# Half two's up-projections and the down-projection of a decoder step by Strassen's scheme

## The chip, the cores and the metric

The kernel runs on one core of a Trainium2 chip. The metric is the device time of one execution in microseconds. Five engines work side by side, each through its own list of instructions in order: TensorE (PE in the profile; its weight loads are a separate line, PEld), VectorE (DVE), ScalarE (ACT), GpSimd (POOL) and SyncE (SP), on whose queue this kernel issues all of its transfers. They hand over by semaphores.

## What is computed

One step of a decoder layer for 2048 prompt tokens and 8 sequences of 4 sample tokens, in float32. Only the end of the layer matters here: a gated feed-forward block (model width 1024, hidden width 2816) behind the token mixer and its output projection, and a last norm.

```python
x = x + g1 * (o @ p['w_out'][l])
h = _rmsnorm(x, p['norm_ffn'][l]) * (1 + sc2) + sh2
gate, b_ffn = _causal_dwconv(h @ p['ffn_w_gate'][l], b_ffn, p['ffn_conv_w'][l])
gate = gate + p['ffn_conv_b'][l]
x = x + g2 * ((jax.nn.silu(gate) * (h @ p['ffn_w_up'][l])) @ p['ffn_w_down'][l])
...
y = _rmsnorm(x, final_norm)
```

## The kernel before, in words

Every dense product is float32 made from three passes: both operands are split into a high part in the type float32r (a cast on ScalarE) and a low part, what is left (a subtraction on VectorE, `raw - hi`), and TensorE adds high·high, high·low and low·high in PSUM. A matmul has a stationary operand of 128 x 128 and a moving one of up to 512 columns.

The tokens go in two halves of 1024. The list of dense blocks that `drive` (L97) walks is `A0 + A1 + B0 + C0 + B1 + C1`: input projections of the halves, output projection of half one (B0), up-projections of half one (C0), output projection of half two (B1), up-projections of half two (C1). The recurrences are woven in as background work up to the end of C0. Behind the list comes `ffn_down` (L1802).

- **B1** (`wout`, L1634). Token tiles of 128 rows; the output weight lies on chip as three groups of columns in the "ring". For each tile the product goes times the gate on VectorE (L1682), plus the residual on GpSimd (L1683), to DRAM as `x1` (L128, the store helper), and is then normed, transposed on TensorE (`prep_turn`, L508) and stored as `h2T`, features by tokens.
- **C1** (`ffn_up`, L1745). The ring holds the half's normalised tokens in three groups of 384, 384 and 256+32 columns (`load_group`, L555, loads them from `h2T`, casts and subtracts). For each of 22 blocks of 128 hidden features there are two weights, gate and up; for each group of tokens `fgroup` (L590) issues 8 x 3 matmuls (L598 to L600). The gate goes through a convolution (`conv_evac`, L656: copies on ScalarE and GpSimd, two multiply-adds on VectorE), tanh and multiply (L652, L653), and times the up product (L1767) it is stored as `aT`.
- **Down** (`ffn_down`). Two passes over all 16 token tiles, each with 11 of the 22 row blocks of `w_down` on chip, 512 columns wide. `a_raw` is loaded, cast (L1899) and subtracted (L1900) per tile; `down_mm` (L1793) issues the matmuls (L1797 to L1799). A tile's sum goes times the gate (L1917, VectorE), plus `x1` (L1918, GpSimd), back to `x1` in pass one, and through the last norm (L1848, L158, L159, L1858) to the output in pass two. The 32 sample rows have products of their own (L1818).

Order in an engine's list is settled when the program is built: code order, rearranged by a scheduler that runs its own estimate of a timeline. Waits are on semaphores between tiles' writers and readers.

Of the kernel before, what the change touches and what calls it, by code (L numbers as in the profile page):

```python
# [31 lines left out]
# groups of tokens (first token, tokens, samples' tokens) of the two halves: the samples go through the input  # L32
# projection with the first half and through the rest with the second
# [11 lines left out]
RA = 4 * (32 * 256 + 32)    # room of a chunk: its four diagonal blocks and the next chunk's are equally far apart  # L45
# [3 lines left out]
class Block:  # L49
    """dense work that shares weight units: loaders of the units, slots of products, what goes between them"""  # L50
# [16 lines left out]
class Kern:  # L67
    def __init__(self, ctx, tc, ins, outs):
        self.ctx, self.tc, self.nc = ctx, tc, tc.nc
        self.i = ins  # L70
        self.o = outs
        self.dram = {}
        self.queue = []
        self.clock = 0
        self.bg = [[], []]      # background work, on the two sides
        self.acc = [0.0, 0.0]
        self.rate = (0, 0)
        self.R = [None] * 3

    # ---------------------------------------------------------------- background and dense work  # L80
# [9 lines left out]
    def finish(self, gens):  # L90
        """emit the background work up to the end of gens"""
# [5 lines left out]
    def drive(self, blocks):  # L97
        """dense blocks, their units loaded ahead, the background work woven in"""
# [24 lines left out]
    # ---------------------------------------------------------------- helpers  # L123
# [6 lines left out]
    def later(self, n, fn):  # L130
        """emit fn behind the n-th next slot of dense products"""
# [23 lines left out]
    def rpow(self, out, in_, n, scale, m):  # L155
        """out = (in*scale + eps) ** -0.5 on small tiles"""
# [4 lines left out]
    # ---------------------------------------------------------------- set up  # L161
    def setup(self):
# [3 lines left out]
        self.pstat = ctx.enter_context(tc.tile_pool(name="pstat", bufs=1, side="left"))  # L166
        self.pw = ctx.enter_context(tc.tile_pool(name="pw", bufs=3, side="left"))
# [35 lines left out]
    def setup2(self):  # L203
        """parameters needed first"""
# [4 lines left out]
        def rows(name, spec):  # L209
            """parameters as rows of 128, transposed on the chip into columns"""  # L210
# [19 lines left out]
    def setup3(self):  # L230
        """masks, the other parameters, persistent states"""
# [7 lines left out]
        self.tri = pc.tile([128, 128], F32, name="tri")  # L239
        nc.gpsimd.affine_select(out=self.tri, in_=self.ones, pattern=[[1, 128]], compare_op=ALU.is_ge,  # L240
                                fill=0.0, base=0, channel_multiplier=-1)
        # blk4[s, t] = 1 in the same block of four tokens; tri4 = blk4 * (s <= t)
        self.tri4 = pc.tile([128, 128], F32, name="tri4")
# [6 lines left out]
        self.blk4 = pc.tile([NS, NS], F32, name="blk4")  # L250
        nc.gpsimd.tensor_copy(self.blk4, self.tri4[:NS, :NS])
        nc.gpsimd.tensor_tensor(self.tri4, self.tri4, self.tri, op=ALU.mult)
        self.neg = pc.tile([128, 128], F32, name="neg")
        nc.vector.tensor_scalar(self.neg, self.tri, 1.0, -NEG, op0=ALU.subtract, op1=ALU.mult)
        self.neg4 = pc.tile([128, 128], F32, name="neg4")
        nc.vector.tensor_scalar(self.neg4, self.tri4, 1.0, -NEG, op0=ALU.subtract, op1=ALU.mult)
        # masks of the HGRN levels in blocks of 32 tokens: second halves as columns, first halves as partitions
        self.lmask = {}
        def quarters(name, src, n):
            """the blocks of n columns on the diagonal of src, under one another"""  # L260
            d = pc.tile([128, n], F32, name=name, tag=name)
# [5 lines left out]
        for h in (1, 2, 4, 8, 16):  # L267
            nb = 64 // h
            m = self.pw.tile([128, 520], F32, name="lm_f", tag="raw", bufs=NRAW)[:, :64]
# [8 lines left out]
        # sel[:, b] = ones in column b  # L278
        self.sel = pc.tile([128, 8, 32], F32, name="sel")
# [13 lines left out]
        # conv weights of the half-argument (silu(x) = y (1 + tanh y), y = x / 2)  # L293
# [3 lines left out]
        # persistent conv halos and states  # L297
        self.halo = pc.tile([128, 14, 3], F32, name="halo")
# [3 lines left out]
        self.sconv = pc.tile([128, 14, 24], F32, name="sconv")  # L302
# [5 lines left out]
        self.Shg = [pc.tile([128, 2, 128], F32, name=f"Shg{n}", tag=f"Shg{n}") for n in range(2)]  # L308
# [1917 lines left out]
```

## Time and profile before

| | |
|---|---|
| three runs, median (lowest to highest) | 2857.83 us (2856.66 to 2860.53) |
| the profiled execution, first to last instruction | 2864.5 us |
| TensorE busy | 2793.7 us, 98% |
| VectorE / ScalarE / GpSimd busy | 1582.8 / 1113.9 / 543.5 us |
| up-projections of half two (C1), from the last matmul of B1 to the first of down | 514.2 us |
| down-projection, to its last matmul | 512.9 us |

In rows of instructions the columns are start, duration, engine, line, operation, output<-inputs, shape and count; in square brackets stands how long the engine was idle before it and for whom. "Busy" of TensorE is a union of overlapping spans: a matmul of 512 columns has a span of about 0.39 us, but they start about 0.23 us apart, so what a matmul costs in a full stream is the distance between starts.

### The profile page before, as it was taken

The numbers are of one execution on the slowest core, as the hardware profiler recorded it, in microseconds if no ns is written. First come the engines' busy times: TensorE is split into PE (matmuls) and PEld (weight loads), VectorE is DVE, ScalarE is ACT, GpSimd is POOL, SyncE is SP. The second block draws the span as 40 slices with busy tenths as digits, with TensorE's granted clock in tenths as the row PEclk, the third lists the DMA queues.
The fourth block names the chain that finished last, engine by engine and source line by source line (L and its number), as shares of the span: only waits on it lengthen the run. The fifth ranks groups of instructions, "written<-read, shape, count | busy, mean of one in ns | idle before, by whom it ended". The sixth has DMA issues, their size and how long they took to land.

```text
span 2864.5 us, 52500 instructions
## 1 busy us (share of the span) xinstructions
PE 2793.7 (98%) x19657; PEld 2555.0 (89%) x19657; DVE 1582.8 (55%) x3434; ACT 1113.9 (39%) x2480; POOL 543.5 (19%) x1143
## 2 busy tenths in 40 slices
PE   7999999999999999999999999999999999999998
PEld 4999888889989999999999989999999997777777
DVE  4535776676576878565565546644434543325433
ACT  4544445445554545544443323432223331113111
POOL 3310222301113322111121102210000002111222
PEclk8999998999999999999999999999999999999999
DMA  6465336675556786553554345632222333345332
GB/s 232 146 201 154 115 108 184 187 214 142 170 177 185 235 271 194 158 153 114 179 160 112 100 142 171 186 100 69 70 68 82 100 114 123 104 141 174 98 117 96
DMA packets 521701, 418.59 MB, mean 146 GB/s; under 512 B 84566, under 2 KB 482806, under 8 KB 520422
## 3 DMA queue, kind: packets, MB, share of 16 engines
q1 hardware_dynamic: 521446, 415.24, 48.0%
q8 instruction: 154, 2.52, 0.4%
q14 instruction: 101, 0.83, 0.1%
HBM read 281.99 MB, written 133.14 MB: 145 GB/s over the span
## 4 chain that ended last, share of the span: by engine, by line
PE 66%; DMA 7%; DVE 3%; issue 1%; ACT 1%; SPq 1%; POOL 0%; DVEq 0%; POOLq 0%; ACTq 0%
PE mm_f L598 13%; PE mm_f L600 13%; PE mm_f L599 13%; PE mm_d L1797 5%; PE mm_d L1799 5%; PE mm_d L1798 5%; DMA rb<-rows 1%; DMA w_raw<-oT 1%; SPq L125 1%; DMA h_raw<-h2T 1%; DMA h_raw<-in_w_out_dram 1%; DMA kq<-qkvT 1%; PE kvt L1031 1%; DMA d_raw<-in_ffn_w_down_dram 1%; PE ssq L717 1%
## 5 line engine op out<-in xcount | busy, mean ns | idle before, releaser
L598 PE MATMUL mm_f<-g_hi,w_hi 128*128 128x384 f32 (+2 forms) x3072 | 1005.8, 327 | 4.2 <-ACT g_hi L569 4.0
L600 PE MATMUL mm_f<-g_hi,w_lo 128*128 128x384 f32 (+2 forms) x3072 | 995.1, 324 | 0.0
L599 PE MATMUL mm_f<-g_lo,w_hi 128*128 128x384 f32 (+2 forms) x3072 | 994.0, 324 | 0.3 <-DVE g_lo L570 0.2
L598 PEld LDWEIGHTS mm_f<-g_hi,w_hi 128*128 128x128 f32 x3072 | 581.1, 189 | 26.0 <-issue 14.8
L599 PEld LDWEIGHTS mm_f<-g_lo,w_hi 128*128 128x128 f32 x3072 | 581.3, 189 | 6.6 <-issue 4.8
L600 PEld LDWEIGHTS mm_f<-g_hi,w_lo 128*128 128x128 f32 x3072 | 581.3, 189 | 6.4 <-issue 5.7
L546 DVE TENSOR_TENSOR w_lo<-w_raw,w_hi 128x512 fp32r<-128x512 f32 (+1 forms) x328 | 228.0, 700 | 132.6 <-ACT w_hi L545 127.6
L545 ACT CAST w_hi<-w_raw 128x512 fp32r<-128x512 f32 (+1 forms) x328 | 201.1, 619 | 240.7 <-PE mm_f L599 196.4
L1797 PE MATMUL mm_d<-d_hi,a_hi 128*128 128x512 f32 (+1 forms) x715 | 282.9, 396 | 1.2 <-ACT d_hi L1789 1.2
L1798 PE MATMUL mm_d<-d_lo,a_hi 128*128 128x512 f32 (+1 forms) x715 | 278.7, 390 | 0.5 <-DVE d_lo L1790 0.5
L1799 PE MATMUL mm_d<-d_hi,a_lo 128*128 128x512 f32 (+1 forms) x715 | 278.6, 390 | 0.0
L671 DVE SCALAR_TENSOR_TENSOR uy<-cv_u,par,uy 128x384 f32<-128x384 f32 (+1 forms) x264 | 151.5, 574 | 196.8 <-ACT uy L668 169.2
L663 ACT COPY cv_u<-mm_f 128x384 f32<-128x384 f32 (+1 forms) x216 | 95.3, 441 | 332.0 <-PE mm_f L600 330.5
L1899 ACT CAST a_hi<-a_raw 128x512 fp32r<-128x512 f32 (+1 forms) x96 | 55.9, 585 | 357.4 <-DMA a_raw<-aT 265.7
L673 POOL COPY fhalo<-cv_u 128x2 f32<-128x2 f32 x132 | 39.8, 301 | 745.2 <-ACT cv_u L663 738.9
L1900 DVE TENSOR_TENSOR a_lo<-a_raw,a_hi 128x512 fp32r<-128x512 f32 (+1 forms) x96 | 68.5, 718 | 193.1 <-ACT a_hi L1899 193.0
L1797 PEld LDWEIGHTS mm_d<-d_hi,a_hi 128*128 128x128 f32 x715 | 134.3, 188 | 38.6 <-issue 4.9
L1799 PEld LDWEIGHTS mm_d<-d_hi,a_lo 128*128 128x128 f32 x715 | 134.5, 188 | 31.1
L1798 PEld LDWEIGHTS mm_d<-d_lo,a_hi 128*128 128x128 f32 x715 | 134.4, 188 | 30.2 <-DVE d_lo L1790 1.3
L1918 POOL TENSOR_TENSOR d_y<-d_y,d_x 128x512 f32<-128x512 f32 x62 | 89.8, 1468 | 369.0 <-DVE d_y L1917 369.0
L641 PE MATMUL mm_t<-w_hi,g_hi 128*128 128x260 f32 (+1 forms) x544 | 141.3, 295 | 4.4 <-ACT g_hi L1967 4.4
L671 DVE SCALAR_TENSOR_TENSOR qy<-cv_u,par,qy 128x384 f32<-128x384 f32 (+1 forms) x216 | 122.8, 572 | 38.5 <-POOL cv_u L662 23.5
(514 smaller groups left out, 4461.3 us busy)
## 6 DMA issues: line engine op xcount, KB each, us to landing
w_raw<-in_w_in_dram SPq DMA_DIRECT2D x96, 256.0 KB
w_raw<-in_ffn_w_gate_dram SPq DMA_DIRECT2D x92, 256.0 KB
w_raw<-in_ffn_w_up_dram SPq DMA_DIRECT2D x92, 256.0 KB
aT<-uy SPq DMA_DIRECT2D x88, 192.0 KB
ada_w<-in_w_ada_dram SPq DMA_DIRECT2D x32, 512.0 KB
R<-recB SPq DMA_DIRECT2D x16, 1024.0 KB
a_raw<-aT SPq DMA_DIRECT2D x64, 256.0 KB
d_x<-x SPq DMA_DIRECT2D x32, 512.0 KB
```

What stands on the lines that cost most here:

```text
L545: nc.scalar.copy(hi[:, :n], raw[:, :n])
L546: nc.vector.tensor_sub(lo[:, :n], raw[:, :n], hi[:, :n].bitcast(F32))
L598: nc.tensor.matmul(ps[:, :N], wh, hi[:, k, :N], start=(k == 0), stop=False)
L599: nc.tensor.matmul(ps[:, :N], wh, lo[:, k, :N], start=False, stop=False)
L600: nc.tensor.matmul(ps[:, :N], wl, hi[:, k, :N], start=False, stop=(k == 7))
L641: nc.tensor.matmul(ps[:m, :nc_], a, wh[:, k % 2], start=(k == 0), stop=False)
L663: nc.scalar.copy(u[:, K:K + n], ps[:, :n])
L671: nc.vector.scalar_tensor_tensor(y[:, :n], u[:, j:j + n], cw[:, j, blk:blk + 1], y[:, :n], op0=ALU.mult, op1=ALU.add)
L1797: nc.tensor.matmul(d, a, hi[:, cs], start=(k == ks[0]), stop=False)
L1798: nc.tensor.matmul(d, a, lo[:, cs], start=False, stop=False)
L1799: nc.tensor.matmul(d, b, hi[:, cs], start=False, stop=(k == ks[-1]))
L1918: (nc.vector if last else nc.gpsimd).tensor_tensor(y[:, cs], y[:, cs], x[:, cs], op=ALU.add)
```

## The change

Strassen's scheme makes the product of two 2 x 2 block matrices from seven block products instead of eight, with sums of blocks as operands and sums of products as results. The form here is Winograd's. Both operands of a product are cut in two both ways:

- **Up (half two only).** A set is two blocks of hidden features (rows) by the two halves of the 1024 model features; the tokens are two groups of 528, each cut into 2 x 264 columns. Each product is 4 x 3 matmuls of 264 columns for each group. The first pair of blocks is done plainly, with eight products to each of four sets; the ten other pairs have two sets each (gate, up), of seven products for both groups.
- **Down.** Three passes, over 8, 8 and 6 row blocks of `w_down` (`KH = (4, 4, 3)`, twice). A set is 256 tokens by 1024 columns, cut in two both ways: each product is `kh` x 3 matmuls of 512 columns. The first set of each pass is plain, seven are Strassen sets.

The combinations of the stationary operand (weights in up, activations in down) are made by `s_combo` on GpSimd, four to a set, of the raw tiles before the split. Those of the moving operand (tokens in up, `w_down` in down) are made by `t_combo` once, two of four on GpSimd and two on VectorE, while the plain sets run; the fourth combination (T4) takes the place of a tile that only the plain sets need. Products 6, 7 and 4 go on adding into the PSUM bank that product 1 began, product 3 into that of product 5; in between ScalarE copies the bank out (`snap`). VectorE joins the copies with later banks (`after`).

```diff
+    def s_combo(q, P, new, eng):
+        t = eng.tensor_tensor
+        if P == "5":
+            q["s"] = new()
+            t(q["s"], q["21"], q["22"], op=ALU.add)
+        elif P == "6":
+            t(q["s"], q["s"], q["11"], op=ALU.subtract)
+        elif P == "3":
+            t(q["12"], q["12"], q["s"], op=ALU.subtract)
+        elif P == "7":
+            t(q["21"], q["11"], q["21"], op=ALU.subtract)
+        return q[{"2": "12", "1": "11", "5": "s", "6": "s", "3": "12", "7": "21", "4": "22"}[P]]
...
+    def s_prod(self, ps, u, T, start):
+        hi, lo = u
+        n = len(T)
+        for k, (th, tl) in enumerate(T):
+            f = dict(stop=False, skip_group_check=True)
+            self.nc.tensor.matmul(ps, hi[:, k], th, start=(start and k == 0), **f)
+            self.nc.tensor.matmul(ps, hi[:, k], tl, start=False, **f)
+            self.nc.tensor.matmul(ps, lo[:, k], th, start=False, stop=(k == n - 1), skip_group_check=True)
...
+        def step(s, P):
+            b = {"2": "Y", "5": "V", "3": "V"}.get(P, "X")
+            seq.append((s, P, P, P, b, P in "215", P))
...
+            step(s, "2")
+            if last:
+                step(s - 1, "4")
+            for P in "15637":
+                step(s, P)
...
+                    if f.pos < len(order) and (f.pos < self.nw or uses[order[f.pos - self.nw]] < f.step):
+                        f.made[order[f.pos]] = unit(*order[f.pos])
...
+        sets = [(k, 0, (g,)) for g in (0, 1) for k in "gu"]
+        n_plain = len(sets)
+        sets += [(k, j, (0, 1)) for j in range(1, NFB // 2) for k in "gu"]
...
+        def unit(s, P):
+            src = raws[s][P] if s < n_plain else self.s_combo(raws[s], P, raw, nc.gpsimd)
...
+                    q = {n: load(g, c, n, new) for n in ("12", "11", "22", "21")}
+                    yield
+                    for P in "567":
+                        put_t(g, c, P, self.t_combo(q, P, new, nc.gpsimd if P == "5" else nc.vector))
+                        yield
+                    r = self.t_combo(q, "4", new, nc.gpsimd)
...
+    def down_tiles(self, pts, n, freed):
...
+            while x[1].replace("B", "4") not in freed:
+                yield
+            put_t(x[1], x[2], raws.pop(x))
...
+        while not {"5", "6", "7"} <= freed:
+            yield
+        last = []
+        for k in range(kh):
+            q = {x: load(x, k) for x in ("12", "11", "22")}
+            r = q["21"] = self.t4.tile([128, 512], F32, name="t4r", tag="t4r", bufs=4)
...
+            for P in "567":
+                put_t(P, k, self.t_combo(q, P, new, nc.gpsimd if P == "5" else nc.vector))
+            last.append(self.t_combo(q, "4", new, nc.gpsimd))
...
+            if P[0] == "C" or P == "4":
+                y, ps = sn(), c[PLAIN_BANK[P] if P[0] == "C" else "X"]
+                nc.vector.tensor_tensor(y, ps, g[:, cs], op=ALU.mult)
+            else:
+                y = c[{"1": "s1", "3": "s6", "7": "s5"}[P]]
+                nc.vector.tensor_tensor(y, c[{"1": "Y", "3": "V", "7": "X"}[P]], y, op=ALU.add)
+                nc.vector.tensor_tensor(y, y, g[:, cs], op=ALU.mult)
+            (nc.vector if s == len(sets) - 1 else nc.gpsimd).tensor_tensor(y, y, x, op=ALU.add)
...
-        self.drive(A0 + A1 + B0 + C0 + B1 + C1)
-        self.flush()
+        self.drive(A0 + A1 + B0 + C0 + B1)
```

Small things around it: masks and recurrence states move to a pool that is closed before half two; the small state outputs that were stored during C1 are stored during the down passes; the weight tiles are prepared four ahead (`SW = 4`); the ring is not loaded for half two, its space is taken by the tokens' operand tiles, whose raw data (`t_raw`) are loaded behind the end of `drive`. Counted in the built program, TensorE has 3744 matmuls of 264 columns where it had 2112 of 384 and 1056 of 288 in C1, and 1881 of 512 columns in down where it had 2079 of 512 and 66 of 256. GpSimd gets 164 operand combinations for the stationary side and 30 for the moving side.

The first place is SyncE's list at the end of B1, before: the stores of a tile's residual (`x_78`, that is `x1`) and the loads of the tokens for the next blocks (`h_raw`).

```order
L125 DMA h_raw<-h2T 128x4x128 x3
L128 DMA h2T<-pr_h 128x8x128
L125 DMA h_raw<-h2T 128x4x128 x6
L125 DMA w_raw<-in_ffn_w_gate_dram 128x4x128 x2
L128 DMA x_78<-wo_y 128x1024
```

And now, at the same place, with the loads called `t_raw`:

```order
L135 DMA h2T<-pr_h 128x8x128
L135 DMA x_78<-wo_y 128x1024
L132 DMA w_raw<-in_ffn_w_gate_dram 128x4x128 x4
L135 DMA x_78<-wo_y 128x1024
L132 DMA t_raw<-h2T 128x2x264 x6
L132 DMA w_raw<-in_ffn_w_up_dram 128x4x128 x4
```

The first load of tokens now stands behind the last tile's store of `x1`; before, the first two groups' loads stood ahead of the last two of these stores.

The second place is TensorE's list at the same point, before:

```order
L1679 MATMUL mm_o<-g_hi,w_hi 128x256
L1680 MATMUL mm_o<-g_lo,w_hi 128x256
L1681 MATMUL mm_o<-g_hi,w_lo 128x256
L598 MATMUL mm_f<-g_hi,w_hi 128x384
L599 MATMUL mm_f<-g_lo,w_hi 128x384
```

And now, where `s_y` and `s_x` are the banks of the first two plain products and `pr_p` the transposes of the last two tiles:

```order
L1690 MATMUL mm_o<-g_lo,w_hi 128x256
L1691 MATMUL mm_o<-g_hi,w_lo 128x256
L524 MATMUL pr_p<-ident,wo_x 128x128 x16
L1827 MATMUL s_y<-t_hi,w_hi 128x264
L1827 MATMUL s_x<-t_hi,w_hi 128x264
L1828 MATMUL s_y<-t_lo,w_hi 128x264
```

The matmuls that followed the last one of B1 at once are now preceded by all the transposes of the last two tiles, and need tokens that are loaded after it.

The third place is GpSimd's list in the last pass of down, before (`d_y,d_x` adds the residual, `d_s` are the small steps of the last norm):

```order
L1918 TENSOR_TENSOR d_y<-d_y,d_x 128x512 x2
L158 TENSOR_SCALAR d_s<-d_s 128x1
L159 TENSOR_TENSOR d_s<-d_s,mhalf 128x1
L158 TENSOR_SCALAR d_s<-d_s 32x1
L159 TENSOR_TENSOR d_s<-d_s,mhalf 32x1
```

And now, where `a_raw` are the combinations of the activations (lines of `s_combo`):

```order
L1794 TENSOR_TENSOR a_raw<-a_raw 128x384
L1800 TENSOR_TENSOR a_raw<-a_raw 128x384
L2313 TENSOR_TENSOR d_y<-d_y,d_x 128x512
L1796 TENSOR_TENSOR a_raw<-a_raw 128x384
L2280 TENSOR_TENSOR d_s<-d_s 128x1
L1798 TENSOR_TENSOR a_raw<-a_raw 128x384
L165 TENSOR_SCALAR d_s<-d_s 128x1
L2313 TENSOR_TENSOR d_y<-d_y,d_x 128x512
L166 TENSOR_TENSOR d_s<-d_s,mhalf 128x1
```

Between a residual's addition and the next stands now a combination that a later product waits for.

## Prediction before the result

> **What bounds the kernel now.** First the page's header, busy shares, the granted clock in 40 slices and the chain that ended last.
>
> ```profile
> span 2864.5 us, 52500 instructions
> PE 2793.7 (98%) x19657; PEld 2555.0 (89%) x19657; DVE 1582.8 (55%) x3434; ACT 1113.9 (39%) x2480; POOL 543.5 (19%) x1143
> PEclk8999998999999999999999999999999999999999
> PE 66%; DMA 7%; DVE 3%; issue 1%; ACT 1%; SPq 1%; POOL 0%; DVEq 0%; POOLq 0%; ACTq 0%
> ```
>
> TensorE is busy 98% of the span and is two thirds of the chain. That average says little of the stages changed, so next the busy time in windows: C1, down, and what follows the last matmul (columns: window, its length, busy time and count of PE, PEld, DVE, ACT, POOL, then clock, DMA share, GB/s).
>
> ```profile
> 1830.04:2344.26 514.22, 513.47 (x3201) 512.80 (x3200) 234.00 (x460) 167.73 (x324) 50.56 (x201) 1.00 0.29 88
> 2344.26:2857.18 512.92, 511.17 (x2345) 401.66 (x2343) 200.41 (x260) 91.05 (x161) 103.71 (x95) 1.00 0.40 126
> 2857.18:2864.50 7.32, 0.00 (x0) 0.00 (x0) 1.73 (x4) 1.23 (x3) 0.93 (x3) 0.85 0.19 72
> ```
>
> Here TensorE waits 0.8 us in C1 and 1.8 us in down, at full clock, and no other engine is half busy. These 1027 us are matmul time, so fewer matmuls shorten them, up to what the new work on the other engines makes TensorE wait.
>
> **What a matmul costs.** From the timeline: a run of 384 columns that starts at 2019.82 and ends where 288 columns begin, the 288s up to the next 384, 24 of 256 columns, and 49 of 512.
>
> ```profile
> 2019.82 0.34 PE L598 MATMUL mm_f<-g_hi,w_hi 128*128 128x384 f32 x1
> 2036.59 0.29 PE L598 MATMUL mm_f<-g_hi,w_hi 128*128 128x288 f32 x1
> 2042.96 0.33 PE L598 MATMUL mm_f<-g_hi,w_hi 128*128 128x384 f32 x1
> 1074.27 0.28 PE L1679 MATMUL mm_o<-g_hi,w_hi 128*128 128x256 f32 x1
> 1077.11 0.28 PE L960 MATMUL gr<-kq_h 128*128 128x256 f32 x1
> 2413.59 0.39 PE L1799 MATMUL mm_d<-d_hi,a_lo 128*128 128x512 f32 x1
> 2424.72 0.40 PE L1799 MATMUL mm_d<-d_hi,a_lo 128*128 128x512 f32 x1
> ```
>
> 96 starts in 16.77 us are 174.7 ns (384 columns), 48 in 6.37 us are 132.7 ns (288), 24 in 2.84 us are 118.3 ns (256), 48 in 11.13 us are 231.9 ns (512). So cost follows columns, without a floor at 256. The new 264 lies between 118.3 and 132.7; I interpolate 121.9 ns (the ends move the sum by -13 and +40 us; it is nearest to 256).
>
> **Matmuls removed.** C1: 22 blocks of (16.77 + 6.37) us = 509.1 us; after, 3744 x 121.9 ns = 456.4 us, **52.7 less**. Down: 2079 x 231.9 + 66 x 118.3 ns = 489.9 us (the other 23 us are sample products and transposes, which stay); after, 1881 x 231.9 = 436.2 us, **53.7 less**. Seven products for eight would be 12.5%; plain sets and narrower matmuls leave 10.6%. 2864.5 - 106.4 = 2758.1 us, if nothing new waits.
>
> **The handoff B1 to half two.** The first tokens are now loaded behind the last tile's store (places one and two above). Prices: the last matmul of B1 and its follower, VectorE, GpSimd and SyncE on such a tile, and from the chain a load of `h2T`.
>
> ```profile
> 1829.76 0.28 PE L1681 MATMUL mm_o<-g_hi,w_lo 128*128 128x256 f32 x1
> 1829.88 0.34 PE L598 MATMUL mm_f<-g_hi,w_hi 128*128 128x384 f32 x1
> 1834.04 0.42 DVE L1682 TENSOR_TENSOR wo_y<-mm_o,g 128x256 f32<-128x256 f32 x1
> 1834.80 0.74 POOL L1683 TENSOR_TENSOR wo_y<-wo_y,wo_x 128x256 f32<-128x256 f32 x1
> 1835.57 0.34 SPq L128 DMA_DIRECT2D x<-wo_y  x1
> 1823.66 3.56 DMA h_raw<-h2T
> 1828.62 4.13 DMA h_raw<-h2T
> L545 ACT CAST w_hi<-w_raw 128x512 fp32r<-128x512 f32 (+1 forms) x328 | 201.1, 619 | 240.7 <-PE mm_f L599 196.4
> ```
>
> 0.42 + 0.74 + 0.34 + 0.34 (issue) + 3.8 + 0.62 (cast) = 6.3 us, about 7 with the handovers; before, the follower started 0.12 us later. The transposes standing ahead need less: their norm chain runs beside the load. Such an idle time costs twice, as an earlier handoff shows (row of TensorE, window):
>
> ```profile
> 1060.86 1.94 PE L514 MATMUL pr_p<-ident,wo_x 128*128 128x128 f32 x8 [5.27 <-DVE wo_x L1653]
> 1060.10:1066.90 6.80, 6.04 (x24) 6.08 (x25) 3.68 (x10) 1.28 (x3) 0.06 (x1) 0.50 0.86 287
> ```
>
> After 5.27 us idle TensorE ran at half clock for 6.8 us, so 6.04 busy us did the work of 3.0. I take 7 + 3, less 0.5 of C1's old waits: **+9.5** (5 to 14). The Trainium skill ("TensorE: Matmul & The Clock Gate", Part 1) says that an idle window of about 3.4 us halves the clock and one busy window restores it; that would lose 1.7 us and give 8.2, but the row shows two windows, and it decides.
>
> **The other engines' new work.** Casts and subtractions hide while they stay ahead: units are made four products ahead, 11.1 us at 12 matmuls of 231.9 ns. The question is one resource. Two pairs of overlapping rows:
>
> ```profile
> 1815.74 1.01 POOL L1683 TENSOR_TENSOR wo_y<-wo_y,wo_x 128x384 f32<-128x384 f32 x1 [1.42 <-DVE wo_y L1682]
> 1815.76 1.54 DVE L570 TENSOR_TENSOR g_lo<-h_raw,g_hi 128x512 fp32r<-128x512 f32 x1
> 1735.35 0.68 DVE L584 TENSOR_TENSOR g_lo<-h_raw,g_hi 128x512 fp32r<-128x512 f32 x1
> 1735.52 1.39 POOL L1683 TENSOR_TENSOR wo_y<-wo_y,wo_x 128x384 f32<-128x384 f32 x1 [10.88 <-DVE wo_y L1682]
> ```
>
> A VectorE subtraction takes 0.68 us alone and 1.54 beside a GpSimd addition, ending 0.55 after it; the addition, 1.01 alone, ends 0.88 after the subtraction in the second pair. They exclude each other but for about 0.13 us. Further prices:
>
> ```profile
> L1918 POOL TENSOR_TENSOR d_y<-d_y,d_x x62: 1273/1300/1753, 2363.2 to 2843.1; 128x512 f32<-128x512 f32 x62
> 1734.88 0.55 DVE L1682 TENSOR_TENSOR wo_y<-mm_o,g 128x384 f32<-128x384 f32 x1
> 2846.50 1.28 DVE L1858 SCALAR_TENSOR_TENSOR d_y<-d_y,d_s,fn 128x1024 f32<-128x1024 f32 x1 [4.06 <-POOL d_s L159]
> ```
>
> Down after: GpSimd 170 operations of 512 (56 and 22 combinations, 92 residuals) x 1.30 and 28 of 384 x 1.01 = 249 us; VectorE with both inputs in SBUF, 279 of 512 x 0.68, 53 of 384 x 0.55, 32 norms x 0.64 = 239 us. Together 488 us by whole durations, 421 with 0.13 off each of the 512 operations, against TensorE's 436 + 23 = 459. So on average it fits, 92% full, and in places not:
> - **Last pass.** A set is 63 matmuls, 14.6 us; the shared resource 4 x 0.88 + 4 x 1.17 + 7 x 0.42 + 3 x 0.55 + 4 x 0.51 = 14.8 us less its slack, 17.6 by whole durations. Seven sets lose 0 to 21 us; I take **10**, since VectorE's and GpSimd's in-order lists can't always interleave.
> - **Three pass starts.** The last row block's combination 5 is needed after ten products, 28 us plus 3 of sample products. Each of four rounds loads four tiles (3.8 us, then 1 us each at 271 GB/s, the highest slice below), combines (1.30), casts (0.62) and subtracts (0.68): first ready about 11 us into the pass, the others about 6.5 us apart: 31 us, even. I take 5 each, **15** (0 to 36).
> - **Up, plain to Strassen.** Four rounds of some 8.5 us against 29 us (16 products of 1.46, two for both groups): **4** (0 to 10). Steady up pairs: nothing, from the rows of C1's VectorE below. A pair of blocks (14 products x 2 groups x 12 x 121.9 ns = 41 us) puts on the resource 14 subtractions x 0.69, 8 combinations x 1.30, and per block what C1 has over its 22: (54.4 + 21.3 + 10.9 + 24.6 + 9.5) / 22 = 5.5, twice; 31 us of 41.
>
> ```profile
> L546 DVE TENSOR_TENSOR w_lo<-w_raw,w_hi 128x512 fp32r<-128x512 f32 x89 | 61.5, 691 | 58.1 <-ACT w_hi L545 58.0
> L671 DVE SCALAR_TENSOR_TENSOR uy<-cv_u,par,uy 128x384 f32<-128x384 f32 x88 | 54.4, 619 | 144.8 <-ACT uy L668 139.5 <-DMA aT<-uy 2.6 <-POOL cv_u L662 1.3
> L653 DVE SCALAR_TENSOR_TENSOR uy<-ut,uy 128x384 f32<-128x384 f32 x44 | 24.6, 558 | 24.5 <-ACT ut L652 24.5
> ...
> L671 DVE SCALAR_TENSOR_TENSOR uy<-cv_u,par,uy 128x256 f32<-128x256 f32 x44 | 21.3, 485 | 4.2 <-ACT uy L668 1.6
> L682 DVE SCALAR_TENSOR_TENSOR uy<-cv_s,par,uy 128x32 f32<-128x32 f32 x44 | 10.9, 247 | 0.0
> ...
> L653 DVE SCALAR_TENSOR_TENSOR uy<-ut,uy 128x288 f32<-128x288 f32 x21 | 9.5, 451 | 0.0
> ```
>
> And what the transfers moved in each of the 40 slices:
>
> ```profile
> GB/s 232 146 201 154 115 108 184 187 214 142 170 177 185 235 271 194 158 153 114 179 160 112 100 142 171 186 100 69 70 68 82 100 114 123 104 141 174 98 117 96
> ```
>
> - **End.** The last piece is 512 columns where it was 256: **+1**. State outputs move from C1 to down, the same transposes: nothing.
>
> Sum: 2758.1 + 9.5 + 10 + 15 + 4 + 1 = 2797.6. The profiled execution is 6.7 us above the median of the runs (2857.8), so **2791 us**.
>
> **Rivals.**
> 1. *The shared resource bounds all of down.* If an operation holds it for its whole duration, down takes 488 us in place of 459, and the pass starts come on top: 2797.6 - 10 + 29 = 2817, less 6.7 **2810**; with starts at their upper bound 2831. For it: the 1.54 us row. Against it: the 0.13 us of overlap, and a GpSimd operation that writes while VectorE reads PSUM waits for nobody. The Trainium skill ("SBUF — State Buffer", Who interferes with whom) has this rule: the port pair is locked for the whole instruction and the other side blocks fully, and two SBUF inputs suffice; the rows agree nearly, not to the last 0.13 us.
> 2. *Nothing waits but the handoff* (lookahead covers the rest): 2758.1 + 5 - 6.7 = **2756**. Against it: the three places above where time is even.
> 3. *Slower: the four-ahead preparation fails.* Products 6 and 3 need chains GpSimd, ScalarE, VectorE, GpSimd (1.30 + 0.62 + 0.68 + 1.30) in order lists that also hold PSUM copies. Of 164 stationary combinations, each exposed adds up to 1.30 us: half of them 107 us, **2898**. It decides from 66 us (0.4 us for each), where the time passes 2857.8. Against it: chains of 3.9 us in 11 us of lead (8.3 in the last pass).
> 4. That the change doesn't do what it says is excluded by the counts of the built program (3744, 1881); narrower matmuls at 288's price would cost 40 us: 2831, inside the range.
>
> **How the numbers follow.** Forecast (2770 to 2805) 0.5; rival 1 with rival 4's price (2805 to 2850) 0.27; rival 2 0.1; slower 0.1; 0.03 near no change. The range 2750 to 2850 leaves out rival 3, the unchanged case and little else. 0.2% is 5.7 us, about what measurement can tell from no change: faster (under 2852) 0.86, same 0.04, slower 0.1.
>
> **What would show it.** Up from 514 to about 475 us with TensorE idle some 7 us at its start and a stretch of clock 0.5 behind it; 264 columns starting 122 ns apart in steady sets. Down at about 485 us: TensorE waits at three pass starts for `t_hi` or `t_lo`, and in the last pass for units whose combination GpSimd made late. VectorE's subtractions in down should average well above 0.69 us. Wrong it would be if TensorE waits in steady sets of the first two passes or of up, above all for the bank copies of ScalarE, or if 264 columns cost more than 133 ns.

## The result, and the profile after

| | before | changed |
|---|---|---|
| runs, median (lowest to highest) | 2857.90 us (2856.66 to 2860.53), 4 runs | 2835.77 us (2830.40 to 2837.89), 4 runs |
| ratio, 95% interval | | 0.9915 (0.9901 to 0.9930) |
| profiled execution | 2864.5 us | 2836.2 us |

Faster by 22 us, where 67 were forecast. The profiled executions differ by 28 us (forecast: 67), so the missing part, 39 us, must show in the trace. First the changed kernel's header, busy shares and granted clock.

```profile
span 2836.2 us, 54513 instructions
PE 2712.0 (96%) x19969; PEld 2466.8 (87%) x19969; DVE 1883.1 (66%) x3771; ACT 1266.5 (45%) x2795; POOL 896.0 (32%) x1338
PEclk8999999999999999999999999999999999999989
```

TensorE fell from 98% to 96% busy: it waits now. Windows tell where: B1's last product to the first of up; up's first 521 matmuls; the rest of up; the Strassen sets of pass one, two and three of down; what follows the last matmul (columns as before).

```profile
1826.99:1835.73 8.74, 2.85 (x18) 2.42 (x16) 5.82 (x12) 5.44 (x11) 3.27 (x9) 0.83 1.07 330
1835.73:1910.00 74.27, 68.28 (x523) 65.70 (x522) 63.69 (x94) 41.51 (x80) 27.12 (x29) 0.97 0.81 239
1910.00:2304.43 394.43, 394.43 (x3231) 394.16 (x3231) 284.09 (x499) 186.75 (x362) 165.46 (x210) 1.00 0.28 85
...
2328.10:2485.60 157.50, 148.18 (x645) 113.61 (x644) 115.47 (x134) 54.22 (x95) 89.28 (x60) 0.98 0.62 187
...
2512.80:2659.90 147.10, 142.59 (x624) 112.80 (x623) 100.11 (x128) 49.78 (x89) 86.20 (x59) 0.99 0.60 183
...
2682.00:2826.43 144.43, 117.36 (x443) 87.19 (x441) 118.21 (x143) 57.37 (x136) 93.64 (x103) 0.92 0.42 135
2826.43:2836.20 9.77, 0.09 (x1) 0.00 (x0) 4.03 (x6) 1.33 (x4) 0.93 (x3) 0.65 0.28 107
```

I take from each length its matmuls at the distances between starts (512 columns 0.2319 us, 264 columns 0.1219, transposes 0.109, sample products 0.10). What is left is TensorE's **loss**, by waits and by half clock: handoff 7.0 us, up's first 521 matmuls 10.8, the rest of up 0.1, pass one 15.4, pass two 7.2, pass three **42.1** (144.4 for 441 x 0.2319 = 102.3). The plain set that begins each pass loses 0.5 or less. Up, 477.4 us with its handoff, is 37 shorter than C1; down, 522.0, is **9 us longer** than before, with 264 fewer matmuls.

What TensorE waited for in pass three (waiting matmul, releaser; us, times, longest), and one of the longer of these waits as a timeline over the engines concerned:

```profile
PE d_ps L1827 <- ACT d_y L2269: 12.0, 7, 4.8
PE d_ps L1829 <- DVE w_lo L1819: 7.2, 6, 2.3
PE d_ps L1827 <- DVE d_y L2311: 3.4, 2, 2.6
PE d_ps L1827 <- ACT w_hi L1818: 3.3, 5, 1.8
PE d_ps L1828 <- DVE t_lo L1819: 1.2, 1, 1.2
```

```profile
2691.18 1.60 POOL L2313 TENSOR_TENSOR d_y<-d_y,d_x 128x512 f32<-128x512 f32 x1
2691.57 1.62 DVE L1819 TENSOR_TENSOR w_lo<-a_raw,w_hi 128x384 fp32r<-128x384 f32 x1
...
2692.81 0.63 ACT L2278 ACTIVATE d_x<-d_y 128x512 f32<-128x512 f32 x1 [0.28 <-POOL d_y L2313]
...
2693.44 0.57 ACT L2269 COPY d_y<-d_ps 128x512 f32<-128x512 f32 x1
...
2694.06 0.79 PE L1827 MATMUL d_ps<-t_hi,w_hi 128*128 128x512 f32 x1 [3.65 <-ACT d_y L2269]
```

TensorE waits 3.65 us for a bank copy; in ScalarE's list the copy stands behind the norm's square (L2278), and that waits for GpSimd's residual (L2313), which runs beside a VectorE subtraction of 1.62 us that alone takes 0.55. Two theories come from this.

- **A, the resource.** GpSimd's operations and VectorE's with both inputs in SBUF exclude each other for their whole duration, and pass three needs that resource for longer than its matmuls take. Worked out anew for a set: 4 combinations x 1.01 + 4 residuals x 1.30 + 7 subtractions x 0.55 + 3 gate products x 0.68 + 4 norm products x 0.74 + two norms' small steps on GpSimd, 2 x (0.19 + 0.19 + 0.55) = 19.9 us; the matmuls take 14.6.
- **B, the queue.** ScalarE's list is in the wrong order: copies that TensorE needs stand behind squares that can wait.

The small steps' prices (the norm's product of 512 columns alone, 0.74, is in e5's rows below):

```profile
2695.94 0.19 POOL L165 TENSOR_SCALAR d_s<-d_s 128x1 f32<-128x1 f32 x1
2696.22 0.55 POOL L166 TENSOR_TENSOR d_s<-d_s,mhalf 128x1 f32<-128x1 f32 x1
```

### The profile page after: what moved, and what is told of

Same layout as the page of the kernel before. It is cut to its first block, busy times and chain, and to the rows that moved or that the text cites. A ratio compares the mean times of both kernels' runs of the same rounds, so it can differ in the third digit from the quotient of the medians.

```text
span 2836.2 us, 54513 instructions
## 1 busy us (share of the span) xinstructions
PE 2712.0 (96%) x19969; PEld 2466.8 (87%) x19969; DVE 1883.1 (66%) x3771; ACT 1266.5 (45%) x2795; POOL 896.0 (32%) x1338
## 5 line engine op out<-in xcount | busy, mean ns | idle before, releaser
L608 PE MATMUL mm_f<-g_hi,w_hi 128*128 128x384 f32 (+2 forms) x2016 | 663.5, 329 | 2.9 <-ACT g_hi L579 2.9
L609 PE MATMUL mm_f<-g_lo,w_hi 128*128 128x384 f32 (+2 forms) x2016 | 653.2, 324 | 0.3 <-DVE g_lo L580 0.2
L610 PE MATMUL mm_f<-g_hi,w_lo 128*128 128x384 f32 (+2 forms) x2016 | 653.0, 324 | 0.0
L608 PEld LDWEIGHTS mm_f<-g_hi,w_hi 128*128 128x128 f32 x2016 | 382.2, 190 | 24.5 <-issue 14.8
L1827 PE MATMUL d_ps<-t_hi,w_hi 128*128 128x512 f32 x627 | 255.1, 409 | 25.3 <-ACT d_y L2269 13.4
L1828 PE MATMUL d_ps<-t_lo,w_hi 128*128 128x512 f32 x627 | 251.8, 402 | 5.2 <-DVE t_lo L1819 5.1
L1829 PE MATMUL d_ps<-t_hi,w_lo 128*128 128x512 f32 x627 | 246.3, 403 | 7.5 <-DVE w_lo L1819 7.5
L1827 PE MATMUL s_x<-t_hi,w_hi 128*128 128x264 f32 x704 | 201.0, 286 | 1.9 <-ACT t_hi L1818 1.0
L1828 PE MATMUL s_x<-t_lo,w_hi 128*128 128x264 f32 x704 | 201.0, 286 | 0.0
L1829 PE MATMUL s_x<-t_hi,w_lo 128*128 128x264 f32 x704 | 199.9, 284 | 0.6 <-DVE w_lo L1819 0.6
L2313 POOL TENSOR_TENSOR d_y<-d_y,d_x 128x512 f32<-128x512 f32 x92 | 141.2, 1536 | 116.2 <-DVE d_y L2312 49.4
L1829 PEld LDWEIGHTS d_ps<-t_hi,w_lo 128*128 128x128 f32 x627 | 120.4, 192 | 39.8 <-DVE w_lo L1819 10.8
```

Of the source, the lines that this page charges most:

```text
L608: nc.tensor.matmul(ps[:, :N], wh, hi[:, k, :N], start=(k == 0), stop=False)
L609: nc.tensor.matmul(ps[:, :N], wh, lo[:, k, :N], start=False, stop=False)
L610: nc.tensor.matmul(ps[:, :N], wl, hi[:, k, :N], start=False, stop=(k == 7))
L1827: self.nc.tensor.matmul(ps, hi[:, k], th, start=(start and k == 0), **f)
L1828: self.nc.tensor.matmul(ps, hi[:, k], tl, start=False, **f)
L1829: self.nc.tensor.matmul(ps, lo[:, k], th, start=False, stop=(k == n - 1), skip_group_check=True)
```

## The experiments

| run | median us | ratio to before (95%) |
|---|---|---|
| e1 residual of pass three on VectorE | 2824.70 | 0.9868 (0.9848 to 0.9888) |
| e2 bank copies of pass three on VectorE | 2837.55 | 0.9915 (0.9892 to 0.9937) |
| e3 pass three plain | 2804.00 | 0.9798 (0.9775 to 0.9822) |
| e4 store of `x1` later | 2833.84 | 0.9900 (0.9882 to 0.9919) |
| e5 residual and combinations on VectorE | 2813.27 | 0.9834 (0.9820 to 0.9849) |
| e6 without the norm's small steps | 2825.12 | 0.9873 (0.9858 to 0.9888) |
| e7 e3 and two plain sets first | 2792.00 | 0.9759 (0.9739 to 0.9778) |
| e8 e7 with three Strassen sets in pass three | 2798.46 | 0.9780 (0.9766 to 0.9795) |
| e9 e7 with all state outputs | 2791.49 | 0.9755 (0.9738 to 0.9771) |
| e10 down all plain | 2820.18 | 0.9858 (0.9841 to 0.9875) |
| e11 the changed kernel again | 2836.19 | 0.9912 (0.9896 to 0.9928) |

The end of B1, ahead of everything changed, lay between 1816 and 1827 us in these profiles, which adds to the spread of the times; between the changed kernel and its repetition (e11) the stages behind it agree within some 3 us, so I read the stages.

**e1.** In pass three the residual's engine is changed:

```diff
-            (nc.vector if s == len(sets) - 1 else nc.gpsimd).tensor_tensor(y, y, x, op=ALU.add)
+            (nc.vector if n == len(KH) - 1 else nc.gpsimd).tensor_tensor(y, y, x, op=ALU.add)
```

> The residual of the last pass is added on VectorE (0.68 us) instead of GpSimd (1.29 us); the kernel changed else stands (2835.8 us). Theory A (GpSimd's operations and VectorE's operations with both inputs in SBUF exclude each other for their whole duration, and the last pass needs that resource for about 19 us a set where TensorE needs 14.6): 26 additions x 0.61 us less on the resource, 16 us: 2820. Theory B (the bank copies of ScalarE stand behind the norm's squares in its list, and these wait for GpSimd's residual): the squares wait for VectorE's list instead, 0 to 8 us less: 2828 to 2836.

Its window of pass three's Strassen sets:

```profile
2681.30:2813.40 132.10, 115.02 (x443) 86.21 (x441) 115.00 (x169) 55.93 (x134) 55.61 (x73) 0.92 0.46 146
```

132.1 us instead of 144.4: 12 of A's 16, and more than the 8 that B allows. The median, 2824.70, lies between the two forecasts. VectorE has 26 additions more (x169 for x143) and is busy for 3 us less.

**e2.** The copies `snap` of pass three by `nc.vector.tensor_copy`:

```diff
-                c["s" + P] = snap(c["V" if P == "5" else "X"])
+                c["s" + P] = snap(c["V" if P == "5" else "X"], nc.vector.tensor_copy if n == len(KH) - 1 else nc.scalar.copy)
```

> The bank copies of the last pass are made by VectorE instead of ScalarE, all else as in the kernel changed. A: the copies read PSUM and do not use the resource; nothing gained, and VectorE's list is 21 x 0.68 = 14 us longer: 2834 to 2846. B: TensorE's 12.0 us of waits for ScalarE's copies go, and half of the clock's loss of 12 us with them: about 2818.

```profile
2675.10:2826.20 151.10, 121.44 (x443) 90.68 (x441) 129.84 (x166) 47.12 (x115) 91.26 (x103) 0.88 0.41 131
```

7 us longer. The copies no longer stand behind the squares, and nothing is gained. TensorE's wait for them grows from 12.0 to 22.3 us:

```profile
PE d_ps L1827 <- DVE d_y L2269: 22.3, 8, 5.7
```

So the delay surfaces at the copies whichever engine makes them, and ScalarE's order by itself is not the cause. The run does not clear that order altogether, since VectorE's list, which now holds the copies, is the longer for them; a ScalarE list with the copies ahead of the squares was not tried.

**e3.** Pass three without the scheme, its combinations skipped:

```diff
-        plain = lambda s: sets[s][1] == 0
+        plain = lambda s: sets[s][1] == 0 or sets[s][0] == len(KH) - 1
...
+            if n < len(KH) - 1:
+                for P in "567":
+                    put_t(P, k, self.t_combo(q, P, new, nc.gpsimd if P == "5" else nc.vector))
+                last.append(self.t_combo(q, "4", new, nc.gpsimd))
```

> The third pass of down does all eight sets with eight products; it makes no combinations of either operand. 8 x 72 x 0.2319 = 133.6 us and 5 us of sample products instead of the 165.1 us from 2661.4 to 2826.5. A: the resource needs about 12 us of each 16.7 us set, nothing waits, 26 us less: 2810. B: no bank copies are left either, so about the same, 2810 to 2815. A rival to both (the norms themselves, squares, small steps and stores, bound the pass): 2825 to 2840.

Its last seven sets:

```profile
2673.00:2790.70 117.70, 117.04 (x505) 94.16 (x503) 62.90 (x91) 32.77 (x86) 50.90 (x70) 1.00 0.49 159
```

504 matmuls x 0.2319 = 116.9 us: nothing waits, at full clock. With 63 matmuls more, the sets take 27 us less; the rival that the norms themselves bound the pass falls.

**e4.** The stores of the last two tiles' `x1` are put off:

```diff
-            self.st(self.dram["x1"][t:t + m, :], y[:m])
+            def x1_out():
+                self.st(self.dram["x1"][t:t + m, :], y[:m])
+            if half == 1 and t >= SEQ - 256:
+                self.later(6, x1_out)
+            else:
+                x1_out()
```

> The x1 stores of half one-sided last two token tiles (tiles 14 and 15) come six steps later, so that the first loads of tokens for the up-projections stand ahead of the last of them on SyncE's queue; the transposes of the last tile then stand behind the first products. Theory of the handoff as predicted (the load stands behind the store, and the store behind the residual): the 7.0 us that TensorE loses between the last product of B1 and the first of up become about 3.5, and the half clock after it (about 3 us) goes or shrinks: 2829 to 2832. Rival (the load waits for the ring's release or for free DMA anyway): 2835 to 2837.

SyncE's queue in the changed kernel, then in e4 with ScalarE's first cast of tokens, and e4's window from B1's last product to the first of up:

```profile
1826.00 2.66 SPq L132 DMA_DIRECT2D w_raw<-in_ffn_w_gate_dram  x4
1829.34 0.34 SPq L135 DMA_DIRECT2D x<-wo_y  x1
1829.73 3.93 SPq L132 DMA_DIRECT2D t_raw<-h2T  x6
```

```profile
1820.35 2.66 SPq L132 DMA_DIRECT2D w_raw<-in_ffn_w_gate_dram  x4
1823.07 3.41 SPq L132 DMA_DIRECT2D t_raw<-h2T  x6
...
1828.12 0.63 ACT L1823 CAST t_hi<-t_raw 128x528 fp32r<-128x528 f32 x1
```

```profile
1821.35:1828.80 7.45, 1.21 (x10) 0.86 (x8) 5.41 (x11) 4.72 (x10) 3.28 (x9) 0.75 1.05 307
```

A miss for both expectations. The loads passed the store, but start 1.7 us after B1's end instead of 2.7, since four weights take 2.66 us to issue ahead of them, and are cast 5 us later, while the DMA engines are full (share 1.05). The loss is 6.6 us instead of 7.0.

**e5.** e1, and the four combinations on VectorE too:

```diff
-            src = raws[s][P] if plain(s) else self.s_combo(raws[s], P, lambda: raw()[:, :128 * kh], nc.gpsimd)
+            src = raws[s][P] if plain(s) else self.s_combo(raws[s], P, lambda: raw()[:, :128 * kh], nc.vector if sets[s][0] == len(KH) - 1 else nc.gpsimd)
```

> In the last pass both the four combinations of a set and the residuals are made by VectorE; GpSimd keeps only the norm's small steps. Theory A (the shared resource bounds the last pass): by whole durations a set needs 13.8 us of VectorE with both inputs in SBUF and 1.9 of GpSimd, 15.6 instead of 19.9, and VectorE alone, with its reads of PSUM, 16.5: seven sets take 116 to 126 us instead of 144.4; time about 2812 (2808 to 2820). Rival (what matters is only that GpSimd's residuals came late, which the run with the residual on VectorE has already taken away): as that run, 2822 to 2828, or worse, since VectorE's list is longer.

Its window, and VectorE's groups there, in the changed kernel first and in e5 behind it (count | busy us, mean ns):

```profile
2677.40:2800.70 123.30, 108.77 (x443) 82.03 (x441) 112.94 (x195) 57.42 (x135) 26.03 (x49) 0.99 0.48 156
```

```profile
L1819 DVE TENSOR_TENSOR w_lo<-a_raw,w_hi 128x384 fp32r<-128x384 f32 x48 | 37.3, 784 | 14.0 <-ACT w_hi L1818 12.7 <-PE d_ps L1829 1.3
L2283 DVE SCALAR_TENSOR_TENSOR d_y<-d_y,d_s,fn 128x512 f32<-128x512 f32 x28 | 30.5, 1131 | 4.8 <-POOL d_s L166 4.8
L2312 DVE TENSOR_TENSOR d_y<-d_y,g 128x512 f32<-128x512 f32 x21 | 18.9, 902 | 0.3
```

```profile
L1819 DVE TENSOR_TENSOR w_lo<-a_raw,w_hi 128x384 fp32r<-128x384 f32 x48 | 27.3, 587 | 2.6 <-ACT w_hi L1818 2.6
L2283 DVE SCALAR_TENSOR_TENSOR d_y<-d_y,d_s,fn 128x512 f32<-128x512 f32 x28 | 19.7, 746 | 1.9 <-POOL d_s L166 1.9
L2312 DVE TENSOR_TENSOR d_y<-d_y,g 128x512 f32<-128x512 f32 x21 | 14.3, 683 | 0.0
```

21 us less, within A's 116 to 126. VectorE does 52 operations more (x195 for x143) and is busy for 5 us less: the same subtraction takes 587 ns without GpSimd beside it and 784 with it. This decides for A: an engine that is done sooner with the other's work added is what a shared resource explains and an order of lists does not. The granted clock of the window rises from 0.92 to 0.99 with it, so up to 10 of the 21 us are half clock that went with the waits.

**e6.** The norm's small steps are dropped:

```diff
-            for i in range(1, n):
-                nc.gpsimd.tensor_tensor(ss[:m, 0:1], ss[:m, 0:1], ss[:m, i:i + 1], op=ALU.add)
-            self.rpow(ss[:m, 0:1], ss[:m, 0:1], 1, 1.0 / D, m)
```

> The last norm's small steps on GpSimd (adding the two halves' sums, scale, power; 3 operations of 128x1 for 128 tokens) are left out, so the outputs are scaled by the first half's sum of squares itself. All else is as in the kernel changed. A, with the small steps as a term that the prediction left out of the resource's sum: 2 x (0.19 + 0.19 + 0.55) = 1.9 us less for each of seven sets, so 8 to 13 us less in the last pass: 2823 to 2829. Rival (operations of one column do not hold VectorE up; what bounds is VectorE's or ScalarE's order): within 4 us of 2835.8.

```profile
2679.70:2812.60 132.90, 110.87 (x443) 84.53 (x441) 114.74 (x144) 55.63 (x135) 74.13 (x54) 0.95 0.46 145
```

11.5 us less: 49 operations on a single column (GpSimd's x54 for x103) are worth nearly as much as e1's move of 26 residuals. They are also a link between the squares and the norm's product, and e6 takes that link away too, so this run alone does not tell the resource from the chain. VectorE's idle time for the chain did not shrink, though: 6.5 us for the steps (L166) in the changed kernel, 10.1 us for the squares here.

**e7.** On e3; passes one and two begin with two plain sets. This kernel makes 20 of the 22 transposes of `ftails` for the small state outputs; the last two and their two stores are left out.

```diff
-        plain = lambda s: sets[s][1] == 0 or sets[s][0] == len(KH) - 1
+        plain = lambda s: sets[s][1] < 2 or sets[s][0] == len(KH) - 1
```

> On top of the last pass with plain sets: passes one and two begin with two plain sets instead of one, so that the moving operand's combinations have another 20 us. Price 2 x 12 matmuls x 0.2319 = 5.6 us. Theory of the pass starts (the even race of 31 us against 31 us is lost: 15.8 us in pass one, 7.2 in pass two): the losses fall to 2 to 5 us and 0 to 1, so 11 to 15 us less than 2804 after the price: 2789 to 2793, or 2795 if pass one keeps half. Rival (pass one's loss is the state outputs' and the sample rows' waits for their own transfers in TensorE's list, whatever the combinations do): 2804 to 2810.

What TensorE waited for in pass one of the changed kernel, and e7's two pass starts:

```profile
PE d_ps L1827 <- ACT t_hi L1818: 3.5, 1, 3.5
PE d_ps L1828 <- DVE t_lo L1819: 2.5, 1, 2.5
PE d_ps L1827 <- ACT w_hi L1818: 1.7, 5, 0.5
```

```profile
2301.20:2351.70 50.50, 49.49 (x253) 36.34 (x252) 36.09 (x43) 15.00 (x26) 25.91 (x17) 1.00 0.82 269
2470.30:2522.60 52.30, 50.66 (x257) 37.58 (x256) 44.40 (x46) 16.56 (x28) 31.25 (x21) 1.00 0.68 224
```

The two starts lose 1.0 and 1.4 us, and the Strassen sets behind them 0.0 and 0.1; 21 us of loss are gone for 24 matmuls (5.6 us); the median falls by 12.0 us from e3's, within the 11 to 15 expected.

**e8.** On e7's pass starts, with all state outputs; Strassen sets at places 2, 4 and 6 of pass three, their residuals on VectorE (the plain block that T4 replaced goes to a free tile):

```diff
-        plain = lambda s: sets[s][1] == 0
+        plain = lambda s: sets[s][1] < 2 or (sets[s][0] == len(KH) - 1 and sets[s][1] % 2 == 1)
```

> As the run before in passes one and two; the last pass has Strassen sets at places 2, 4 and 6 of its eight (numbered from 0) and plain sets at the others, with the residuals of the Strassen sets on VectorE. The plain block that the combination T4 replaced lies in a place that is free in a pass of three. Theory A: a Strassen set needs 17.4 us of the resource and a plain one 12.2, on average 14.1 against 15.9 us of matmuls, so three sets save 9 x 0.2319 = 2.1 us each, 6 us less than the run before (2785). Rival (a Strassen set waits whatever stands beside it, since the units ahead of it are only four): no gain or some us more, 2791 to 2800.

```profile
2684.60:2789.50 104.90, 98.20 (x407) 76.44 (x407) 76.82 (x113) 37.60 (x96) 43.14 (x61) 0.98 0.51 163
```

A miss for A taken as an average. From the first Strassen set on, 405 matmuls are 93.9 us, and 11.0 are lost, 3.7 for each Strassen set, which saves 2.1. Plain neighbours with room on the resource do not help; that units are made only four products ahead would explain it, and was not tried by itself. The trace fits: ahead of the first combination of two of the sets GpSimd stood idle 17.3 us, waiting for VectorE's subtraction of an earlier unit.

```profile
POOL a_raw L1794 <- DVE w_lo L1819: 17.3, 2, 14.7
```

**e9, e10 and e11.** e9 is e7 with the state outputs complete (a step of them behind the second plain set; first diff). e10 has no Strassen set in down at all, in the same three passes (second diff). e11 is the changed kernel on the same chip.

```diff
-            if not plain(s) and q < nq - 1 and P == "6":
+            if q < nq - 1 and P == ("223" if q == 1 and n < len(KH) - 1 else "6"):
```

```diff
-        plain = lambda s: sets[s][1] == 0
+        plain = lambda s: True
```

> The run with two plain sets at the start of passes one and two and a plain last pass, with the small state outputs stored as in the kernel changed (the step that a second plain set took away from them is given back). From the stages so far: down takes about 482 us with 3 us lost; 2792 (2787 to 2797). Rival (the state outputs' transposes and stores disturb the plain sets at the pass start): 2797 to 2803.

> All sets of down with eight products, in the same three passes; up as in the kernel changed. It shows what Strassen's scheme in down is worth by itself, with the new passes. 2112 x 0.2319 = 489.8 us and some 20 us of sample products and transposes, nothing lost: down 512 us where the kernel changed takes 522: 2826. By the prediction (losses of 25 us against 53.6 us of matmuls less) the plain form should be slower than the kernel changed by 28 us or more; by theory A with the pass starts it is faster by 8 to 12 us.

> The kernel changed itself, beside the two others on one chip: 2836 (2830 to 2840), and down's stages as before (passes' Strassen sets lose 15, 7 and 42 us).

Down to its last matmul, e9 and e10:

```profile
2300.70:2781.50 480.80, 477.03 (x2177) 374.24 (x2176) 300.92 (x393) 149.80 (x294) 249.53 (x204) 1.00 0.61 192
```

```profile
2300.40:2809.10 508.70, 506.96 (x2322) 401.50 (x2320) 192.35 (x273) 93.87 (x190) 150.80 (x140) 1.00 0.57 182
```

e11 repeats the changed kernel: pass three loses 43.5 us, pass one 15.7, pass two 9.0. e10, without the scheme in down, is 16 us faster than it (8 to 12 were expected by A; the time, 2820.18, is 6 below the 2826 expected): down's half of the change was a net loss, and the gain that was measured is up's. e9 is faster than both kernels, 45 us below the changed one, with 12 of down's 24 sets by Strassen's scheme.

## Why the prediction was wrong

Sign, stage and matmuls were right, and the time lay in the range; the size was a third of the forecast. By the prediction's own steps:

1. **What bounds, and the matmuls removed: right.** In the rest of up 3223 matmuls of 264 columns and 6 of 512 take 394.43 us, which is 121.9 ns for 264 columns, the interpolated price.
2. **Handoff, +9.5: size right, a link wrong.** 7.0 us of loss and then half clock: 15 matmuls take the 3.77 us between these starts, 1.9 more than at full clock, together 8.9.

```profile
1834.10 1.97 PE L524 MATMUL pr_p<-ident,wo_x 128*128 128x128 f32 x8 [4.15 <-ACT pr_h L538]
...
1835.73 0.59 PE L1827 MATMUL s_y<-t_hi,w_hi 128*128 128x264 f32 x1
...
1839.50 0.30 PE L1829 MATMUL s_y<-t_hi,w_lo 128*128 128x264 f32 x1
```

The store is not what sets it (e4): the weights' issue and the loads' own 5 us take its place. A second chain ends with the loads. TensorE waits 4.15 us for ScalarE's `pr_h`, which empties the bank that the last tile's transposes need, and these run until the first token is cast:

```profile
1835.05 1.36 ACT L1818 CAST t_hi<-t_raw 128x528 fp32r<-128x528 f32 x2 [0.65 <-DMA t_raw<-h2T]
1832.70:1839.50 6.80, 5.40 (x23) 5.09 (x24) 5.92 (x14) 5.59 (x13) 0.00 (x0) 0.50 1.11 348
```

So the transposes did not "need less". In e4 they stand behind the first products, and TensorE waits 4.51 us for the cast instead. Of the clock, the Trainium skill ("TensorE: Matmul & The Clock Gate", Part 1) says that one busy window restores it. The second row has the granted clock at 0.50 for 6.8 us, as long as at the earlier handoff, on which I went; 3.77 us of it lie behind the first product. In both places TensorE was idle when it began (here until 1834.10), so no run here tells two windows from one that is busy throughout.

3. **Up, plain to Strassen, +4: mis-sized.** 10.8 less 1.9 is 8.9, within the bounds given (0 to 10). Of TensorE's waits there 2.4 us are for the moving operand (`t_hi`, `t_lo`), which the sum priced, 2.4 us for the weights (`w_lo`), which it did not, and 0.8 us for a bank copy. Steady pairs lost nothing, as predicted.
4. **Three pass starts, +15: 23** (15.4, 7.2 and 0.5). The mechanism is shown by e7, and by e9 with all state outputs: 20 us more for the combinations take away all but 2.5 us. In pass one TensorE's waits for `t_hi` and `t_lo` stand where they were foretold. In pass two they are 1.4 us, and the longest wait is of another kind, a sample product's for its weights:

```profile
PE mm_ds L2220 <- DMA t_raw<-in_ffn_w_down_dram: 2.4, 1, 2.4
```

5. **Last pass, +10: the step that failed; it lost 42.1.** The prediction put the resource at "14.8 us less its slack, 17.6 by whole durations" against 14.6 us of matmuls. That sum left out work. I count all rows in the window of GpSimd and of VectorE with two inputs in SBUF, each at its duration when nothing is beside it: 151 us, 21.5 for each of seven sets. What was missing is GpSimd's small steps of the norm (15 us; e6 gains 11.5 us without them), the last of the moving operand's combinations and subtractions, which run into this window (9 us), the sample rows' steps (4 us), and 0.1 us on each norm product, which was taken as half of one with 1024 columns, 0.64 us for 0.74 (3 us); the other terms were 4 us too large. Two groups of these, as they ran (count | busy us, mean ns):

```profile
L166 POOL TENSOR_TENSOR d_s<-d_s,mhalf 128x1 f32<-128x1 f32 x15 | 10.5, 700 | 0.7
L1819 DVE TENSOR_TENSOR t_lo<-t_raw,t_hi 128x512 fp32r<-128x512 f32 x5 | 6.6, 1331 | 0.0
```

The 0.13 us taken off every operation was not the error. One or the other of these rows is at work in 129.7 of the 144.4 us, so 21 of the 151 us overlap, 0.10 for each of 218 operations. That is 18.5 us of the resource a set, where TensorE needs 14.6: the prediction took the pass for bound by TensorE with a little lost, and it is bound by the resource. Its share of the loss is 7 x (18.5 - 14.6) = 27 us, an estimate, which holds if another order of the lists can't overlap more. The other 15 us are waits that the lists add and half clock: (1 - 0.92) x 144.4 = 11.6 us is the most that half clock can have cost, a term that the prediction had at the handoff and not here.
6. **The end, +1: 2.4** (9.77 us for 7.32).

The ledger of the profiled executions: 32.1 (last pass) + 8.1 (pass starts) + 4.9 (up's start) + 1.4 (end) - 0.6 (handoff) = 45.9 us more than forecast. B1 ended 2.9 us earlier, and 4.3 us of C1's and down's old waits, which the forecast kept, are in the losses already: 38.7, against 2836.2 - 2797.6 = 38.6. The medians differ by 6 us less than the profiles, because the profile of before lies 6.6 us above its median and this one 0.4.

Rival 1 had the mechanism but not the place: GpSimd's operations and VectorE's with two inputs in SBUF exclude each other, which e1 and e5 bear out, but the resource bounds pass three and not all of down. The steady sets of passes one and two lose next to nothing once the pass starts have time (e7). The Trainium skill's page "SBUF — State Buffer" (Who interferes with whom) says that the other engine is blocked for the whole instruction. The rows here agree but for the 0.10 us an operation. As a sum over down, rival 1 was also too cheap (2810 to 2831), lacking the same small steps. The case against it, "0.13 us of overlap", was about right in size and did not matter: pass three is over full in spite of it. One of the prediction's sums is off without effect: "421 with 0.13 off each of the 512 operations" lists 562 operations, which gives 415. Rival 2 falls. Rival 3's place, the four-ahead chains, shows in e8 and in the rows of waits for `w_lo`, but passes one and two lost little in their steady sets, so it did not decide. In pass three, as I read it, the combinations were late because the resource was full.

By whole durations a set of pass three and seven of them stand to the measured windows like this: changed 19.9, 139 and 144.4; e6 18.0, 126 and 132.9; e1 17.4, 122 and 132.1; e5 16.5 (VectorE's whole list, now the larger), 116 and 123.3. The sum is always 5 to 10 us short, and always in the right order. That it comes so near is partly luck: in the changed kernel it leaves out 12 us of late combinations and sample rows, and does not take off the 21 us that overlap.

Open: why e8's Strassen sets lose 3.7 us each between plain neighbours; what would shorten the handoff, where only one edit was tried; and how much of pass three the six tiles for results cost, since ScalarE's copies stood idle 5.4 us there until stores of the output gave a tile back, and more tiles were not tried.

## What to carry to other kernels

Where work is moved from TensorE to elementwise engines, add up GpSimd's operations and VectorE's with two inputs in SBUF as one resource, all that the stage's window holds, one-column steps and leftovers of the stage before too (less some 0.1 us an operation, as measured here), and for the stage that carries most of them, not for the average. Mix the scheme: a pass that already carries the norm keeps its eight products, and where operands have to be made first, a second plain set costs 2.8 us and took away 6 to 14 us of loss here. In a table of waits the releaser (here ScalarE's copies) is where a delay comes out; moving it to another list (e2) tests whether it was made there, as far as that list has room.

## What the runs showed of the hardware

One-column operations on GpSimd that take 0.19 and 0.55 us when nothing is beside them took up to 0.64 and 0.99 us in pass three, and dropping 49 of them was worth 11.5 us (e6). Two such rows of GpSimd in the changed kernel, each with an operation of VectorE beside it that ends within 0.1 us of it:

```profile
2688.44 0.64 POOL L2280 TENSOR_TENSOR d_s<-d_s 128x1 f32<-128x1 f32 x1
...
2694.28 0.99 POOL L166 TENSOR_TENSOR d_s<-d_s,mhalf 128x1 f32<-128x1 f32 x1
```

And an engine with more to do can be done sooner: VectorE's busy time in pass three fell from 118.2 us to 112.9 in e5 with 52 operations more, once most of GpSimd's work was out of the way.
